# A hand-synchronised ring of two blocks, a looped TensorE program, and ScalarE sums in every block, for row skewness

## The chip, the cores and the metric

One core of a Trainium2 chip. The metric is the device time of one execution in microseconds (us); times quoted are medians of several executions, with their range. In the profile, PE is the matrix engine (TensorE), PEld its weight load, DVE is VectorE, ACT is ScalarE, POOL is GpSimd, SP the engine that issues the loads. All times inside an execution count from the start of the profile's span.

An execution more than 1.5% above the fastest of the same kernel is marked slow.

## The reference

```python
rows, cols = 1024, 8192                      # x, float32, normal
mean = np.mean(x, axis=-1, keepdims=True)
std = np.std(x, axis=-1, keepdims=True)
z = (x - mean) / (std + 1e-8)
return np.mean(z ** 3, axis=-1)              # 1024 numbers
```

The 33.5 MB of x are read once. From the three raw sums of a row (of x, x^2 and x^3) the result follows in a few small operations.

## The kernel before

Eight blocks of 128 rows by 8192 columns, each loaded in pieces. For every piece ACT squares (and sums the squares), DVE multiplies the square by x (and sums the cubes), and PE sums x: it transposes chunks of 128 columns, all added up in one PSUM tile `tp`; ACT copies that tile, and one more matmul with a column of 1/n gives the mean. A scheduler sets all waits and picks one of eight buffers for each piece.

```python
UNITS = [[4096, 4096], [4096, 4096], [4096, 4096], [4096, 4096],
         [3584, 2304, 2304], [2304, 2304, 2048, 1536],
         [1664, 1792, 1920, 1664, 1152],
         [1024, 1024, 1152, 1280, 1408, 1152, 1152]]
S1_ACT = {(0, 0): 1024, (1, 0): 1024, (2, 0): 1024}   # columns that ACT sums
X_BUFS = 8
# ...
for k, w in enumerate(widths):
    xt = xpool.tile([P, w], FP, tag="x", name=f"x_{b}_{k}")
    nc.sync.dma_start(out=xt, in_=xv[b, :, c0 : c0 + w])
    for s, e in _slices(w):                            # at most 2304 columns
        nc.scalar.activation(out=sq, in_=xt[:, s:e], func=AF.Square, scale=s_scale,
                             accum_out=s2u[:, j : j + 1])
        nc.vector.scalar_tensor_tensor(out=cube, in0=sq, scalar=1.0, in1=xt[:, s:e],
                             op0=ALU.mult, op1=ALU.mult, accum_out=s3u[:, j : j + 1])
    # ... ACT's sum, where S1_ACT has one
    for c in range(n):
        nc.tensor.matmul(out=tp, lhsT=xt[:, c * P : (c + 1) * P], rhs=ident,
                         start=..., stop=..., is_transpose=True)
nc.scalar.copy(out=tsb, in_=tp)                        # once a block
nc.tensor.matmul(out=s1ps[:, b : b + 1], lhsT=tsb, rhs=onesn, start=True, stop=True)
# ... the first six blocks are closed together, the last two on ACT, step by step
```

## Time and profile before

| | before |
|---|---|
| time, median (range) | 91.47 us (91.38 to 91.63), 4 runs |
| span of the profile | 89.7 us |
| 16 DMA engines busy with loads | 89.7% of the span |
| last piece landed | 83.56 us |
| last square on ACT ended | 84.72 us |
| last product on DVE ended | 87.20 us |
| ACT from its first to its last square | 69.0 us busy, 7.6 us idle |
| mean granted clock of PE | 0.978 |

The busy rows of the page cut the span into 40 slices, a digit for each (9 is 90% or more). A row of groups gives line, engine, operation, output<-inputs, count, then busy time and mean length in ns, then the idle time just before these instructions and what ended it. Landing times and the sizes of single packets come from the records in the trace; the row on ACT's busy and idle time was added up from its instruction records. The lines themselves stand in the prediction.

### The profile page before, as it was taken

The numbers are of one execution on the slowest core, as the hardware profiler recorded it, in microseconds if no ns is written. First come the engines' busy times: TensorE is split into PE (matmuls) and PEld (weight loads), VectorE is DVE, ScalarE is ACT, GpSimd is POOL, SyncE is SP. The second block draws the span as 40 slices with busy tenths as digits, with TensorE's granted clock in tenths as the row PEclk, the third lists the DMA queues.
The fourth block names the chain that finished last, engine by engine and source line by source line (L and its number), as shares of the span: only waits on it lengthen the run. The fifth ranks groups of instructions, "written<-read, shape, count | busy, mean of one in ns | idle before, by whom it ended". The sixth has DMA issues, their size and how long they took to land.

```text
span 89.7 us, 1368 instructions
## 1 busy us (share of the span) xinstructions
PE 64.9 (72%) x504; PEld 59.3 (66%) x504; DVE 72.7 (81%) x80; ACT 72.1 (80%) x106; POOL 11.3 (13%) x14
## 2 busy tenths in 40 slices
PE   0003999892882919989998988888987798969710
PEld 0003999791872909979897977877876787848500
DVE  1000498989999298995999999999999999999970
ACT  6003999699991999859898989978979898999950
POOL 3000000000000000000000000000005999900030
PEclk9999999999999997599999999999999999999998
DMA  3999999999999999999999999999999999994000
GB/s 117 351 424 438 424 431 431 431 431 424 446 416 431 424 438 424 424 438 427 415 409 418 419 427 419 421 415 419 409 414 417 404 413 411 421 412 161 0 0 2
DMA packets 4038, 33.64 MB, mean 375 GB/s; under 512 B 576, under 2 KB 576, under 8 KB 2240
## 3 DMA queue, kind: packets, MB, share of 16 engines
q1 hardware_dynamic: 4032, 33.56, 89.7%
q8 instruction: 4, 0.07, 0.3%
q14 instruction: 2, 0.02, 0.0%
HBM read 33.55 MB, written 0.00 MB: 374 GB/s over the span
## 4 chain that ended last, share of the span: by engine, by line
DMA 73%; ACT 13%; issue 5%; DVE 4%; SPq 1%; PE 1%; DVEq 0%; ACTq 0%
DMA x<-in_x_dram 73%; ACT sq L147 9%; DVE sq L152 3%; ACT sqps L147 1%; ACT same L159 1%; SPq L140 1%; PE s1ps L175 1%; ACT tsb L174 0%; ACT s3u L128 0%; ACT v L127 0%; ACT var L125 0%; DVE num L189 0%; ACT m1sq L124 0%; DVE skew L192 0%; ACT nm L126 0%
## 5 line engine op out<-in xcount | busy, mean ns | idle before, releaser
L152 DVE SCALAR_TENSOR_TENSOR sq<-sq,x 128x2048 f32<-128x2048 f32 (+9 forms) x35 | 70.7, 2071 | 13.4 <-ACT sq L147 13.3
L165 PE MATMUL tp<-ident,x 128*128 128x128 f32 x488 | 62.6, 288 | 17.3 <-DMA x<-in_x_dram 17.2
L165 PEld LDWEIGHTS tp<-ident,x 128*128 128x128 f32 x488 | 57.9, 150 | 20.9 <-DMA x<-in_x_dram 12.7
L147 ACT ACTIVATE sq<-x 128x2048 f32<-128x2048 f32 (+9 forms) x35 | 60.6, 1734 | 10.7 <-DMA x<-in_x_dram 9.9
L110 POOL TENSOR_TENSOR vara<-m2a,m1sqa 128x6 f32<-128x6 f32 x1 | 1.8, 1822 | 67.1 <-DVE m3a L99 67.1
L147 ACT ACTIVATION_READ_ACCUMULATOR sq<-x 128x1 f32 x35 | 6.5, 186 | 0.0
L175 PEld LDWEIGHTS s1ps<-onesn,tsb 128*128 128x128 f32 x16 | 2.4, 188 | 5.2 <-ACT tsb L174 5.2
L175 PE MATMUL s1ps<-onesn,tsb 128*128 128x1 f32 x16 | 3.1, 260 | 3.3 <-ACT tsb L174 3.3
L174 ACT COPY tsb<-tp 128x128 f32<-128x128 f32 x8 | 2.0, 256 | 2.0 <-PE tp L165 2.0
L114 POOL TENSOR_TENSOR rra<-vara,expo 128x6 f32<-128x6 f32 x1 | 3.3, 3267 | 0.0
L159 ACT ACTIVATE same<-x 128x1024 f32<-128x1024 f32 x3 | 3.1, 1041 | 0.0
L152 DVE DVE_READ_ACCUMULATOR sq<-sq,x 128x1 f32 x35 | 2.9, 83 | 0.0
L111 POOL TENSOR_TENSOR m1sq3a<-m1sq3a,vara 128x6 f32<-128x6 f32 x1 | 1.9, 1868 | 0.1
L77 ACT ACT_TABLE_LOAD x1 | 1.3, 1283 | 0.7 <-PEq L208 0.7
L187 POOL TENSOR_TENSOR rr<-var,expo 128x2 f32<-128x2 f32 x1 | 0.7, 702 | 7.7 <-ACT var L125 7.7
L152 DVE SCALAR_TENSOR_TENSOR cube<-sqps,x 128x1152 f32<-128x1152 f32 x1 | 1.4, 1350 | 0.0
L113 POOL TENSOR_TENSOR m3a<-m3a,m1sq3a 128x6 f32<-128x6 f32 x1 | 1.2, 1201 | 0.1
L147 ACT ACTIVATE sqps<-x 128x1152 f32<-128x1152 f32 x1 | 1.1, 1136 | 0.1
L115 POOL TENSOR_TENSOR skew<-m3a,rra 128x6 f32<-128x6 f32 x1 | 1.1, 1069 | 0.1
L124 ACT ACTIVATE m1sq<-s1ps 128x1 f32<-128x1 f32 x2 | 0.3, 171 | 0.5 <-PE s1ps L175 0.5
L75 DVE MEMSET onesn<- 128x1 f32 x1 | 0.1, 59 | 0.8 <-PEq L208 0.8
L112 POOL TENSOR_TENSOR m1sq3a<-m1sq3a,nm1a 128x6 f32<-128x6 f32 x1 | 0.7, 697 | 0.0
(28 smaller groups left out, 6.8 us busy)
## 6 DMA issues: line engine op xcount, KB each, us to landing
x<-in_x_dram SPq DMA_DIRECT2D x8, 2048.0 KB, 23.4
x<-in_x_dram SPq DMA_DIRECT2D x4, 1152.0 KB, 27.9
x<-in_x_dram SPq DMA_DIRECT2D x4, 576.0 KB, 8.6
x<-in_x_dram SPq DMA_DIRECT2D x1, 1792.0 KB, 33.0
x<-in_x_dram SPq DMA_DIRECT2D x2, 832.0 KB, 13.9
x<-in_x_dram SPq DMA_DIRECT2D x1, 1024.0 KB, 21.1
x<-in_x_dram SPq DMA_DIRECT2D x2, 512.0 KB, 10.0
x<-in_x_dram SPq DMA_DIRECT2D x1, 960.0 KB, 13.2
```

The source lines that it names most:

```text
L77: nc.scalar.activation(out=tiny, in_=onesn, func=AF.Square)
L110: g.tensor_tensor(out=var, in0=m2, in1=m1sq, op=ALU.subtract)
L111: g.tensor_tensor(out=m1sq3, in0=m1sq3, in1=var, op=ALU.add)
L113: g.tensor_tensor(out=m3, in0=m3, in1=m1sq3, op=ALU.add)
L114: g.tensor_tensor(out=rr, in0=var, in1=expo, op=ALU.pow)
L115: g.tensor_tensor(out=skew[:, 0:F], in0=m3, in1=rr, op=ALU.mult)
L147: nc.scalar.activation(out=sq, in_=xt[:, s:e], func=AF.Square, scale=s_scale, accum_out=s2u[:, j : j + 1],)
L152: nc.vector.scalar_tensor_tensor(out=cube, in0=sq, scalar=1.0, in1=xt[:, s:e], op0=ALU.mult, op1=ALU.mult, accum_out=s3u[:, j : j + 1],)
L159: nc.scalar.activation(out=same[:, 0:w_act], in_=xt[:, w - w_act : w], func=AF.Copy, scale=inv_n, accum_out=s1a[:, b : b + 1],)
L165: nc.tensor.matmul(out=tp, lhsT=xt[:, c * P : (c + 1) * P], rhs=ident, start=(k == 0 and c == 0), stop=(c0 == C and c == n - 1), is_transp ...
L174: nc.scalar.copy(out=tsb, in_=tp)
L175: nc.tensor.matmul(out=s1ps[:, b : b + 1], lhsT=tsb, rhs=onesn, start=True, stop=True)
```

## The change

Its intent: do away with the scheduler's waits and with most of PE's instruction stream. The whole of x passes through a ring of two blocks; every engine has one semaphore and a written order; PE runs a loop of four turns over two blocks (110 transposes, 55 a block) and gets "grants" from SP as pieces land. For the loop every block must look alike, so ACT sums the first 1152 columns of every block. Blocks 4 to 7 are cut into fewer pieces, and the closing of a block is rewritten.

```diff
-    [3584, 2304, 2304],
-    [2304, 2304, 2048, 1536],
-    [1664, 1792, 1920, 1664, 1152],
-    [1024, 1024, 1152, 1280, 1408, 1152, 1152],
+    [2304, 2944, 2944],
+    [2176, 1664, 2176, 2176],
+    [1920, 2304, 2304, 1664],
+    [1536, 1920, 1792, 1664, 1280],
 ]
-S1_ACT = {(0, 0): 1024, (1, 0): 1024, (2, 0): 1024}
-X_BUFS = 8
+S1_ACT = 1152
+RING = 2
+ISSUE_LAG = 6000
+PARTS = (
+    [4096, 6144, 7168, 8192],
+    [4096, 6144, 7168, 7680, 8192],
+)
... (a small class that records each engine's operations with the names they wait for)
+    for i, (b, u, s, e) in enumerate(slices):
+        k = units[u][1]
+        square(i)
+        cube(i)
+        pos = i - of_block[b][0]
+        if pos == (1 if b < 4 else 0):
+            first_sum(b)                      # ACT: 1152 columns
+        if b == F and pos == 1:
+            early_on_act()                    # ACT: needs m1a of blocks 4, 5
+        if b and b % RING == 0 and pos == 1 and b <= F:
+            means(b // RING - 1)              # DVE: makes m1a of two blocks
...
+        if i == of_block[b][-1]:
+            copy_sums(b)                      # ACT: needs PE's last part of b
...
+        with tensor.Fori(0, NB // RING):
+            for h in range(RING):
+                c0 = S1_ACT
+                for i, end in enumerate(PARTS[h]):
+                    tensor.sem_inc(more, -1)._wait_ge(more, 1)      # a grant
+                    for c in range(c0, end, P):
+                        t = nc.tensor.matmul(
+                            out=tp[h], lhsT=at(h, c, c + P), rhs=ident,
+                            start=c == S1_ACT, stop=c + P == C, is_transpose=True,
+                        )
+                    t.then_inc(pe, 1)
+                    c0 = end
+                    if h and i == 0:
+                        mean(0)
+            mean(1)
```

In the code F is 6, L is 7 and NB is 8; `m1a` holds the means of the first six blocks, and DVE fills it for two blocks at a time. A part of PARTS is granted when the piece that holds its last column has landed; a piece may be overwritten when its cubes, ACT's sum and PE's part are done.

## The prediction

An assumed time per grant is cut that went into the walk and so into its waits; an assumed stop of PE's loop is cut that stood with the third rival, whose 99 to 101 us now rest on PE's slow pace alone ("its clock" there is PE's).

> **What bounds the kernel now.** I read the page's busy tenths and chain first, then the groups, the waits, the DMA view, and the timeline of the first and last ten microseconds.
>
> ```profile
> DVE  1000498989999298995999999999999999999970
> ACT  6003999699991999859898989978979898999950
> PEclk9999999999999997599999999999999999999998
> DMA  3999999999999999999999999999999999994000
> ...
> DMA 73%; ACT 13%; issue 5%; DVE 4%; SPq 1%; PE 1%; DVEq 0%; ACTq 0%
> ```
>
> The DMA row is full from the second slice to the 36th, and the chain lies on loads for 73% of the span. The load stream is the bound: the last piece lands at 83.56 us (the trace's landing records). ACT and DVE are nearly as full, so the margin below the stream is small. PE's clock drops once, in the slices around 36 to 40 us.
>
> ```profile
> L152 DVE SCALAR_TENSOR_TENSOR sq<-sq,x 128x2048 f32<-128x2048 f32 (+9 forms) x35 | 70.7, 2071 | 13.4 <-ACT sq L147 13.3
> L165 PE MATMUL tp<-ident,x 128*128 128x128 f32 x488 | 62.6, 288 | 17.3 <-DMA x<-in_x_dram 17.2
> L147 ACT ACTIVATE sq<-x 128x2048 f32<-128x2048 f32 (+9 forms) x35 | 60.6, 1734 | 10.7 <-DMA x<-in_x_dram 9.9
> L174 ACT COPY tsb<-tp 128x128 f32<-128x128 f32 x8 | 2.0, 256 | 2.0 <-PE tp L165 2.0
> L159 ACT ACTIVATE same<-x 128x1024 f32<-128x1024 f32 x3 | 3.1, 1041 | 0.0
> ```
>
> What counts here is ACT's idle time. Of its 10.7 us before squares, 5.95 is the wait for the first piece (timeline), leaving 4.8; the copies add 2.0 and two small waits 0.8. Between 8.18 us and the end of the last square at 84.84, ACT therefore idles only some 7.5 us, nearly all of it waiting for data. This is the room that new ACT work can use.
>
> ```profile
> q1 hardware_dynamic: 4032, 33.56, 89.7%
> q8 instruction: 4, 0.07, 0.3%
> q14 instruction: 2, 0.02, 0.0%
> ```
>
> The four q8 packets have 16,384 bytes each and start at 26.3, 47.4, 65.2 and 80.9 us. They look negligible and are not. In the landing records of the piece before the first one, the median DMA engine lands at 22.33 and the last at 22.74; of the next piece, at 27.22 and 28.85. One engine lost 1.2 us to one packet and never won it back[...]. After 47.4 a second engine is 1.2 us late. At the end the median is 81.92 and the last 83.56.
>
> ```profile
> 83.58 1.14 ACT L147 ACTIVATE sqps<-x 128x1152 f32<-128x1152 f32 x1
> 84.84 0.27 ACT L174 COPY tsb<-tp 128x128 f32<-128x128 f32 x1
> 85.24 1.35 DVE L152 SCALAR_TENSOR_TENSOR cube<-sqps,x 128x1152 f32<-128x1152 f32 x1
> 86.44 0.29 ACT L128 ACTIVATE s3u<-v,nm 128x1 f32<-128x1 f32 x1
> 87.04 0.16 DVE L192 TENSOR_TENSOR skew<-num,rr 128x2 f32<-128x2 f32 x1
> 87.23 0.35 SPq L193 DMA_DIRECT2D out_dram<-skew  x1
> ```
>
> The last square starts 0.02 us after its data: ACT is just in time. The end costs 3.6 us after the last landing, up to the end of the last result at 87.20.
>
> [...] PE's 504 weight loads and 504 matmuls make about 1,010 instructions[...] and there are four packets. [...] here transposes are 117 ns apart when warm (32 in 3.71 us), but 214 at the start (28 in 5.99 us), and the drop near 36 us comes in a stretch where PE was 70% busy.
>
> **The change part by part.**
>
> *PE's loop.* One turn is 110 weight loads, 110 transposes, 9 grants and two means of 5 instructions: 239[...]. If it isn't fetched again the four packets go. That is worth 1.64 (81.92 to 83.56) less the 0.41 of natural spread: 1.2 us of landing time.
>
> *Loads.* Packets of 4,608 bytes take 181 ns and of 9,216 bytes 352, so 11 ns fixed and 0.0369 ns a byte; a piece costs an engine 8 x 11 + 9 = 97 ns beyond its bytes. 24 pieces for 27 save 0.3 us. The ring does hold fewer columns, but a place lies free about 6.6 us after its piece landed (two squares, two cubes)[...], and comes round only after 16,384 columns, 19.8 us. I find no starved queue. Estimated last landing: 83.56 - 1.2 - 0.3, about 82.1 to 83.0 (the walk below uses 83.0).
>
> *ACT's work.* From the rows by shape (2048: 1907 ns, 1152: 1155) a square costs 0.84 ns a column + 0.188 us, start to start. Between first landing and end of the last square, after:
> - 34 squares: 8 x 8192 x 0.84 ns + 34 x 0.188 = 61.4 us (36 before: 61.8)
> - 8 sums of 1152 columns at 1.155: 9.2 us (before 3 of 1024 at 1.048: 3.1)
> - 7 copies at 0.28: 2.0; first closing 0.45; six steps of block 6's closing 1.65
>
> The sum is 74.7 us against 69.0 before. Starting at 8.2, ACT can't finish its last square before 82.9 even if it never waits: it has become as long as the load stream.
>
> *ACT's waits.* I walked the four orders (ACT, DVE, PE, SP) of the changed program instruction by instruction, each starting when its engine is free and its waits are met, with the durations above, 1.041 ns a column + 0.10 us for a cube, 117 ns a transpose[...]. The same walk over the order of before, given its landings, ends at 87.36 where the trace has 87.20, so its sums hold to about 0.2 us. For after it gives:
> - Blocks 0 to 3: seven waits of 0.3 to 0.5 us, 2.9 in all. ACT now takes 9.1 us of the 9.9 us of a block.
> - End of block 4: 0.6 us at the copy, which waits for PE.
> - End of block 5: 1.8 us at the copy. The pieces end at 3840, 6016 and 8192, PE's parts at 4096, 6144, 7168, 7680, 8192, so the part to 6144 just misses the third piece, and 32 transposes (3.8 us and four grants) are left after the last one.
> - Block 6: 2.8 us. After the second square ACT needs `m1a` of blocks 4 and 5. On DVE it is queued behind the cube of that very square (2304 columns, 2.5 us). This follows from the order alone and can't be hidden.
>
> 8.2 + 74.7 + 2.9 + 0.6 + 1.8 + 2.8 = 91.0 for the end of the last square (84.84 before), although its data landed at 83.0.
>
> *The end.* Then 0.3 for the last step of block 6, 0.28 for the copy, 0.5 for the mean on PE, 0.6 to the variance, 0.75 for the power on GpSimd, 0.2 for the product: 93.6. DVE's last cube ends at 92.6 and isn't on the path. Before it was 87.2: 6.4 us more. The launch around it should stay as it was: 91.54 + 6.4 = 97.9. I add 0.3 because with 55 transposes a block everywhere PE is about 70% busy, as where its clock dropped, and a slow stretch delays a copy: 98.2.
>
> **The rivals.**
> - *The load stream stays the bound, and the change wins.* Landing 1.5 us earlier with an end of 3.6 to 4.5 us gives 90.0 to 91.0. For it speak the 73% of loads on the chain; against it ACT's sum of 74.7 us, which leaves no room for the end, and the waits above. It needs ACT never to wait.
> - *ACT is the bound but its waits are short* (PE and DVE come in time, 2.9 us of waits alone): 8.2 + 74.7 + 2.9 + 2.7 = 88.5, so 92.9. Against it: the order in block 6.
> - [...] its clock stays low. [...] 214 in place of 117 ns for one part of 23 transposes (2.2 us), reaches ACT through the copies: 99 to 101.
> - *The ring starves the loads.* Loads of block 7 wait for PE's parts and cubes of block 5; if ACT lags by 6 us they are late too. In the walk each is still issued about 11 us or more before it lands, so this costs nothing more.
>
> **Range and chances.** The largest uncertain terms are the three waits (5.2 us) and PE's clock (0 to 2.5 us). Half of the waits gone gives 95.6; a slow PE gives 100.5. The limit for "within 2%" is 93.4, which needs nearly all waits gone. Slower 0.89, same 0.06, faster 0.05.
>
> **What would show each step.** The q8 instruction packets are gone from the middle of the span, and the last landing comes at 82 to 83 us. ACT's sum group has 8 at 1.15 us. The waits show ACT's small square of `m1a` waiting 2.8 us for DVE, and the copies waiting for PE by 4 us or more in all. The last square starts 5 us or more after its data, and the chain shows ACT where it showed loads. It would be wrong if ACT's idle time within the stretch were under 4 us, if the loads landed after 85 us (then the ring is the cause), or if PE's loop stopped for its branch.

## The result

The changed kernel takes **99.63 us** (98.44 to 100.27, 4 runs) against 91.47 us. The ratio is 1.0847 (95% interval 1.0746 to 1.0947). A ratio here is the mean time of one kernel's fast runs over that of the other's of the same rounds, so it isn't quite the ratio of the quoted medians (1.0892). The result lies between the 95.6 and 100.5 that the prediction works out for its good and its bad case, 1.4 us above the predicted 98.2.

The page of the changed kernel, part 2 (busy tenths) and part 4 (the chain); a slow run, 100.27 us:

```profile
DVE  0000798989898949898999998899145909999960
...
ACT  6006999699969696999999979990398099999940
PEclk9999999999999999999999996559999975998555
DMA  4899999999999999999999999999999991000000
...
POOL 1%; ACT 1%; PE 1%; issue 0%; DVE 0%; DVEq 0%; POOLq 0%
```

The DMA row now ends in the 34th slice of a longer span, and behind it there are five slices of work without loads. The chain says little here: it breaks off at 93.38 us and so covers only the last 2.3 us (the shares add up to some 3%), so that it shows neither loads nor ACT as the bound, and the readings below rest on waits and timeline instead. ACT is busy from the fourth slice to the 38th but for shallow dips (the 6s in the row) and two holes, in slices 28 to 29 and 32. PE's clock drops in slices 25 to 27 and 33 to 34, and again at the end where PE has little to do; before it dropped once.

```profile
L343 PE MATMUL tp<-ident,ring 128*128 128x128 f32 x440 | 56.6, 292 | 28.6 <-PEq L341 28.4
L183 ACT ACTIVATE sq<-ring 128x2048 f32<-128x2048 f32 (+8 forms) x34 | 61.2, 1804 | 9.2 <-DMA ring<-in_x_dram 9.2
L200 ACT ACTIVATE same<-ring 128x1152 f32<-128x1152 f32 x8 | 9.2, 1152 | 0.0
L209 ACT COPY tsb<-tp 128x128 f32<-128x128 f32 x8 | 2.1, 260 | 4.8 <-PE tp L343 4.8
L228 ACT ACTIVATE m1sqa<-m1a 128x6 f32<-128x6 f32 x1 | 0.2, 208 | 2.7 <-DVE m1a L216 2.7
```

These are the groups that answer to those of before. The sums cost ACT 9.2 us where they cost 3.1. ACT's wait for data ahead of squares is 9.2 us, 5.96 of it for the first piece, so 3.3 us for all others. New are 4.8 us of waiting for PE at the copies and 2.7 us for DVE ahead of a small square that takes 0.2 us.

```profile
q1 hardware_dynamic: 3600, 33.56, 81.6%
q8 instruction: 1, 0.02, 0.1%
q14 instruction: 2, 0.02, 0.0%
```

In the queues (packets, MB, share of 16 engines) one of the four q8 packets is left; it has 16,384 bytes, starts at 31.3 us and takes 1.08 us. One is enough: in the landing records the last DMA engine comes 0.37 us after the median one for the piece before it (27.52 and 27.89) and 1.5 us after it for the next (32.44 and 33.92), and so to the end (81.98 and 83.45). The last landing is 83.45 us, against 83.56 before: the loads gained 0.1 us in all.

Lines picked from the timeline around blocks 5 and 6 (start, length, engine, line, operation, in brackets the idle time before and who ended it):

```profile
61.05 5.14 PE L343 MATMUL tp<-ident,ring 128*128 128x128 f32 x23 [3.60 <-PEq L341]
...
66.82 3.69 PE L343 MATMUL tp<-ident,ring 128*128 128x128 f32 x32 [0.41 <-PEq L341]
70.55 0.27 ACT L209 COPY tsb<-tp 128x128 f32<-128x128 f32 x1 [4.07 <-PE tp L343]
75.89 2.56 DVE L192 SCALAR_TENSOR_TENSOR sq<-sq,ring 128x2304 f32<-128x2304 f32 x1 [1.09 <-ACT sq L183]
78.37 0.15 DVE L216 TENSOR_TENSOR m1a<-s1ps,s1a 128x2 f32<-128x2 f32 x1
78.56 0.21 ACT L228 ACTIVATE m1sqa<-m1a 128x6 f32<-128x6 f32 x1 [2.71 <-DVE m1a L216]
```

PE stands idle for 3.6 us until the third piece of block 5 has landed (60.88 us), then takes 5.14 us for 23 transposes (the second block's 23 took 2.70), then 3.69 us for the other 32, and ACT, which had squared all of block 5 by 66.5, waits 4.07 us for it. Then the small square of `m1a` waits until the 2.56 us cube ahead of the sum is through.

And lines picked from the end:

```profile
91.59 1.25 ACT L183 ACTIVATE sq<-ring 128x1280 f32<-128x1280 f32 x1
93.03 0.24 ACT L209 COPY tsb<-tp 128x128 f32<-128x128 f32 x1
93.21 1.49 DVE L192 SCALAR_TENSOR_TENSOR sq<-sq,ring 128x1280 f32<-128x1280 f32 x1
94.74 0.70 POOL L292 TENSOR_TENSOR rr<-var,expo 128x2 f32<-128x2 f32 x1 [11.03 <-ACT var L252]
95.55 0.16 DVE L302 TENSOR_TENSOR skew<-num,rr 128x2 f32<-128x2 f32 x1 [0.28 <-POOL rr L292]
```

The last square starts 8.1 us after its data landed; before it was 0.02 us. From its end to the last product it takes 2.9 us (92.84 to 95.71), where the kernel before took 2.5.

### The profile page after: what moved, and what is told of

Same layout as the page of the kernel before. It is cut to its first block, busy times and chain, and to the rows that moved or that the text cites. A ratio compares the mean times of both kernels' runs of the same rounds, so it can differ in the third digit from the quotient of the medians.

```text
span 98.5 us, 1321 instructions
## 1 busy us (share of the span) xinstructions
PE 58.7 (60%) x456; PEld 56.0 (57%) x456; DVE 73.5 (75%) x79; ACT 76.9 (78%) x112; POOL 5.9 (6%) x14
## 5 line engine op out<-in xcount | busy, mean ns | idle before, releaser
L192 DVE SCALAR_TENSOR_TENSOR sq<-sq,ring 128x2048 f32<-128x2048 f32 (+8 forms) x34 | 72.3, 2164 | 20.7 <-ACT sq L183 20.5
L343 PE MATMUL tp<-ident,ring 128*128 128x128 f32 x440 | 56.6, 292 | 28.6 <-PEq L341 28.4
L343 PEld LDWEIGHTS tp<-ident,ring 128*128 128x128 f32 x440 | 53.5, 152 | 30.4 <-issue 30.4
L183 ACT ACTIVATE sq<-ring 128x2048 f32<-128x2048 f32 (+8 forms) x34 | 61.2, 1804 | 9.2 <-DMA ring<-in_x_dram 9.2
L200 ACT ACTIVATE same<-ring 128x1152 f32<-128x1152 f32 x8 | 9.2, 1152 | 0.0
L183 ACT ACTIVATION_READ_ACCUMULATOR sq<-ring 128x1 f32 x34 | 6.4, 188 | 0.0
L235 POOL TENSOR_TENSOR vara<-m2a,m1sqa 128x6 f32<-128x6 f32 x1 | 0.2, 197 | 77.2 <-ACT m1sq3a L229 77.2
L192 DVE DVE_READ_ACCUMULATOR sq<-sq,ring 128x1 f32 x34 | 2.8, 83 | 0.0
L200 ACT ACTIVATION_READ_ACCUMULATOR same<-ring 128x1 f32 x8 | 1.5, 189 | 0.0
L235 POOL TENSOR_TENSOR rra<-vara,expo 128x6 f32<-128x6 f32 x1 | 1.3, 1336 | 0.0
## 6 DMA issues: line engine op xcount, KB each, us to landing
ring<-in_x_dram SPq DMA_DIRECT2D x3, 1088.0 KB, 10.8
```

Source lines behind the costliest of these rows:

```text
L183: pr.op("act", ("sq", i), waits, lambda: act(out=sqs[i % SQ_BUFS][:, 0 : e - s], in_=at(b, s, e), func=AF.Square, scale=s_scale, accum_out ...
L192: pr.op("dve", ("cube", i), [("sq", i), "s3u"], lambda: dve.scalar_tensor_tensor(out=sq, in0=sq, scalar=1.0, in1=at(b, s, e), op0=ALU.mult ...
L200: pr.op("act", ("s1a", b), us + prev, lambda: act(out=same, in_=at(b, 0, S1_ACT), func=AF.Copy, scale=inv_n, accum_out=s1a[:, b : b + 1],))
L235: pr.op("pool", name, waits, lambda: g.tensor_tensor(out=out, in0=in0, in1=in1, op=op))
L343: t = nc.tensor.matmul(out=tp[h], lhsT=at(h, c, c + P), rhs=ident, start=c == S1_ACT, stop=c + P == C, is_transpose=True,)
```

## The experiments

Twelve kernels ran, each timed in three rounds beside the kernel before on the same chip. All give the right result but `no_sums`. The last column is the difference from the changed kernel's ratio, turned into us of 91.5. The change wasn't run again in these rounds, and the interval of its own ratio is 0.9 us either way, so a difference of less than about 1 us in that column can't be told from none.

| kernel | all runs, us (s: marked slow) | ratio to before | against the change |
|---|---|---|---|
| the change | 100.27s, 99.87, 99.39, 98.44 | 1.0847 | |
| means_first | 97.07, 96.93, 96.65, 97.49 | 1.0605 | -2.2 |
| piece_6144 | 99.17s, 97.52, 99.43s, 99.02s | none | unclear |
| piece_4096 | 99.19, 98.93, 98.86, 98.99 | 1.0813 | -0.3 |
| copy_late | 97.63s, 97.40, 97.86s, 96.07 | 1.0573 | -2.5 |
| sum_128 | 97.28, 97.63, 97.43, 97.52 | 1.0632 | -2.0 |
| no_sums | 98.18s, 98.16s, 96.52, 97.59 | 1.0593 | -2.3 |
| unrolled | 99.92s, 99.89s, 97.71, 100.10s | none | unclear |
| warm | 99.61, 99.58, 99.67, 99.84 | 1.0873 | +0.2 |
| before_sums | 93.42, 93.53, 93.38, 93.55 | 1.0195 | (on the kernel before) |
| means_copy | 95.47, 95.15, 94.84, 95.72 | 1.0397 | -4.1 |
| all_fixed | 94.24, 95.01, 94.24, 93.72 | 1.0297 | -5.0 |
| all_fixed_512 | 93.18, 93.92, 94.28, 94.43 | 1.0285 | -5.1 |

### means_first: the wait for DVE

```diff
         square(i)
-        cube(i)
         pos = i - of_block[b][0]
+        if b and b % RING == 0 and pos == 1 and b <= F:
+            means(b // RING - 1)
+        cube(i)
...
-        if b and b % RING == 0 and pos == 1 and b <= F:
-            means(b // RING - 1)
```

> The sum of the means of blocks 4 and 5 on DVE (m1a) is put before the second cube of block 6 instead of behind it; nothing else. Theory (ACT is the bound, its waits add to the end): the 2.7 us wait of ACT's small square for DVE goes and the whole of it comes off the end: 99.6 - 2.7 = about 96.9 us (95.5 to 98.0 with the spread of PE's clock). Rival (the ring or the load stream sets the end): nothing over 0.5 us.

Measured: 97.0 us, 2.6 us less by the medians and 2.2 by the ratios. The group of the small square, in the profile:

```profile
L228 ACT ACTIVATE m1sqa<-m1a 128x6 f32<-128x6 f32 x1 | 0.2, 199 | 0.0
```

Its 2.7 us of idle time are gone, and most of them came off the end. What ACT waits for here sets the end, and an order of two instructions on DVE was worth over 2% of the time.

### piece_6144 and piece_4096: why PE is late in block 5

```diff
-    [2176, 1664, 2176, 2176],
+    [2176, 1664, 2304, 2048],      # piece_6144
+    [2176, 1920, 1920, 2176],      # piece_4096
```

> Block 5 is cut at 2176, 3840, 6144, 8192, so that PE's part to 6144 no longer misses the third piece: the reason that the prediction gave for the 1.8 us wait at the end of block 5. If that reason holds: about 1.5 us faster, 98.1. Rival: PE is late because its first part ends at 4096 and so starts only with the third piece, after which 55 transposes stand without a gap; then the cut changes nothing: 99.6 within 0.7.

> Block 5 is cut at 2176, 4096, 6016, 8192, so that PE's first part starts with the second piece. By the rival reason of the run before, PE is 0.7 us or more nearer to its data, and it idles 2.4 us less ahead of that part, so that its clock need not drop (it took 5.1 us for 23 transposes where 2.7 is usual): the wait of 4.1 us at the copy falls to 1 to 2 us, and the time to 96.7 to 97.5 us. If PE's clock drops all the same: 98.9.

Of piece_6144 only one run counts as fast, so its time settles nothing. Its profile (99.17 us, slow) does: PE's 23 transposes start at 61.61, end at 65.98, and the 32 others follow without a gap. The earlier grant found PE still at work, so a cut at 6144 couldn't bring it forward. The prediction's reason for the wait is wrong.

With the cut at 4096 PE's work is in another order; its timeline:

```profile
55.38 6.20 PE L343 MATMUL tp<-ident,ring 128*128 128x128 f32 x55 [0.68 <-PEq L341]
...
64.40 5.06 PE L343 MATMUL tp<-ident,ring 128*128 128x128 f32 x32 [2.71 <-PEq L341]
```

The 23 transposes of block 5 now run on behind block 4's, as the rival said, and the wait at the copy falls to 1.40 us. But PE then waits for the last piece, and it is the 32 transposes that run slowly (5.06 us for 3.69). Another copy, in block 2, waited 2.8 us in this run. So the time of 98.96 us is what was expected for the case that the clock drops all the same (98.9; 0.88 was granted on average); the gain of 0.3 us is within the noise.

### copy_late: the waits at the copies

```diff
-        if i == of_block[b][-1]:
+        if b and pos == 0:              # behind the first square of block b
+            copy_sums(b - 1)
+            if b - 1 >= F:
+                pending = close_on_act(b - 1)
+        if i == of_block[L][-1]:
             copy_sums(b)
-            if b >= F:
-                pending = close_on_act(b)
+            pending = close_on_act(b)
```

> ACT copies the sums of a block behind the first square of the next block instead of ahead of it, so that ACT doesn't stand still while PE finishes. Theory: the waits at the copies (0.7 and 4.1 us in the profiled run) are hidden by the square: 99.6 - 3.5 = about 96.1 us (95.5 to 97), with less spread from run to run, since PE's clock then hardly reaches ACT. Rival (PE's lag counts anyway, through the places that it frees and the loads that follow): less than 1 us.

Measured: 97.5 us by the median, 2.5 us less by the ratio (96.7 us as mean of its two fast runs). The wait view of its profile (engine, line <- who: us in total, times, longest; a slow run):

```profile
ACT tsb L209 <- PE tp L346: 1.9, 1, 1.9
```

One wait of 1.9 us is left, for block 5, where PE is over 3 us late, more than a square can hide. So the gain is about two thirds of what was expected; the expectation that the scatter would shrink was wrong (96.07 to 97.86).

### sum_128 and no_sums: ACT's own sums

```diff
-S1_ACT = 1152
+S1_ACT = 128                       # sum_128
```
```diff
-        pr.op("act", ("s1a", b), ...)        # no_sums: the sums away,
+        pr.marks["s1a", b] = pr.marks["s1a0"]
+    pr.op("dve", "s1a0", [], lambda: dve.memset(s1a, 0.0))
```

> ACT sums 128 columns of each block instead of 1152, PE's loop has 126 transposes instead of 110. It takes 6.9 us of work from ACT and gives 8 transposes more a block to PE. Theory A (ACT's own sums are the whole of the loss): 99.6 - 5.8 = about 94 us. Theory B (ACT mostly waits for others by now, and PE takes longer with each block, so that the room is turned into longer waits at the copies: 2.1 and 2.9 us by the walk with warm PE, and 0.8 us a block for data): only 0.8 to 2 us, 97.5 to 98.8.

> The changed kernel without ACT's sums (s1a is set to zero on DVE; the result is wrong on purpose, as 1152 columns are missing from each mean). PE's work and all waits stay. This takes 9.2 us of work from ACT, and, unlike sum_128, gives PE nothing more. Theory (by now ACT stands behind PE and DVE in blocks 4 to 6, so what it saves ahead of them it waits there): 99.6 - 2.1 = about 97.5 us (96.5 to 98.5), with the waits at the copies 1.5 to 2 us longer than the 4.8 us of the changed kernel. Rival (the sums are the loss): 93 or less.

Both times land where the second theory put them: 97.48 us (-2.0, at the edge of the range) and, with PE's work unchanged, 97.88 us (-2.3 by the ratio). 9.2 us of work less on ACT bring 2.3 us. Where the rest went stands in the waits of no_sums (a slow run, as the profiled one of the change):

```profile
ACT sq L184 <- DMA ring<-in_x_dram: 11.5, 7, 5.9
ACT tsb L206 <- PE tp L340: 8.4, 5, 3.7
ACT m1sqa L225 <- DVE m1a L213: 2.7, 1, 2.7
```

The copies wait 8.4 us instead of 4.8 (3.6 more, where 1.5 to 2 were expected), the squares 11.5 instead of 9.2, the small square 2.7 as ever. Added up from the records between first and last square, ACT is busy 65.0 us and idle 16.7, where the changed kernel has 73.7 and 10.8: two thirds of the saved work has become waiting. ACT was no longer the engine that everything waits for; it took turns with PE and DVE.

### before_sums: the same kind of sum in the kernel before

```diff
+            if b >= nw and k == 0:          # blocks 3 to 7; the result is not used
+                nc.scalar.activation(
+                    out=same, in_=xt[:, 0:1024], func=AF.Copy, scale=inv_n, accum_out=spare,
+                )
```

> The kernel before with one sum more on ACT in each of blocks 3 to 7 (1024 columns, the result not used), PE's work as it was: 5.2 us of ACT work alone. Theory (ACT is full at the end, so the sums of the last blocks count): 91.46 + 1.9 = 93.3 us (92.8 to 93.8) by the same walk. Rival (ACT waits for data 7.5 us, the sums fit in there): under 0.5 us.

Measured: 93.47 us, ratio 1.0195 (1.0171 to 1.022), so 1.8 us, by the walk 1.9. In a kernel where ACT idles 7.6 us, 5.2 us of work on it still cost a third of themselves. (Not all of this idle time is waiting for data, as the expectation has it: 4.8 us are, 2.0 are waits of the copies for PE.) The chain of this run fits with that:

```profile
ACT 37%; DMA 33%; issue 12%; PE 7%; DVE 5%; SPq 3%; DVEq 0%; ACTq 0%
```

The chain was on loads for 73% before; with the sums it is on loads for a third and on ACT for more.

### unrolled and warm: PE's loop and PE's clock

```diff
-        with tensor.Fori(0, NB // RING):
+        for _ in range(NB // RING):                # unrolled
```
```diff
+                    if i < 2:                      # warm, ahead of a grant
+                        for _ in range(8):
+                            nc.tensor.matmul(out=idle, lhsT=ident, rhs=ident,
+                                             start=True, stop=True, is_transpose=True)
                     tensor.sem_inc(more, -1)._wait_ge(more, 1)
```

> PE's loop is written out, all else the same. One instruction packet of 16 KB is left with the loop and has made one DMA engine 1.1 us late; written out there should be four. As one packet already costs what four cost (each meets another engine), the last landing stays at 83.4 us within 0.3 and the time at 99.6 within 0.8. Rival (the loop's branch or a refetch stops PE): 1 us or more faster. Rival (the packets matter): landing 1 us later.

> In each block PE does eight transposes of the identity into a place that nobody reads ahead of its first and of its second grant, where it would stand idle: 3.7 us more work a turn. Theory (PE's clock drops because PE is 60% busy): the granted clock rises from 0.90 to 0.95 or more, the waits at the copies fall by 2 us or more, the time to 97.0 to 98.0. Rival (the clock has another cause, or the extra work delays PE as much): 99.6 or slower.

Written out, three runs took 99.9 to 100.1 us and one 97.71, so the time can't be told from the loop's (only one run counts as fast). The queue:

```profile
q8 instruction: 3, 0.05, 0.2%
```

Three packets (I had expected four), a last landing of 83.82 us against 83.45 with one packet and 83.56 with the four of the kernel before. So each packet beyond the first cost 0.4 us or nothing. In the landing records of the kernel before, the packet at 47.4 us made a second engine late rather than the late one later: of the 16 engines the last three bring the next piece at 49.39, 50.60 and 50.75 us, and brought the one before it at 46.45, 46.62 and 47.83. The loop neither wins nor loses anything that can be seen.

Warm did what it was meant to do to the clock, 0.95 for 0.90, and nothing to the time, 99.64 us. Its clock row and the line of block 5:

```profile
PEclk9999999999999999999999999589999999999755
...
61.09 4.22 PE L351 MATMUL tp<-ident,ring 128*128 128x128 f32 x23 [2.74 <-PEq L349]
```

The drop that the changed kernel has in slices 33 to 34 is gone, the one at 61 us (slices 26 to 27 here) is not: PE still had to wait 2.74 us for the third piece there, and 23 transposes took 4.22 us. The copy of block 5 waited 3.4 us. So the mean clock is a poor measure here; what costs is one drop in the one place where ACT waits for PE, and filling other gaps didn't help it.

The clock records of the traces of the kernel before and of the changed one show where the drops come, which the mean hides. Before, the clock was half from 34.62 to 38.03 us (and from 89.23, after PE's last work); in the changed kernel from 59.70 to 66.53, from 80.18 to 83.60 and from 90.42 on. In the 3.41 us (the length of the shortest of these) ahead of the drops at 34.62, 59.70, 80.18 and 90.42 PE was busy 40%, 34%, 30% and 32% of the time; in warm it worked 1.04 of the 3.77 us ahead of 61.09 us, 28%. Yet as idle a stretch elsewhere brought none: from 31.20 to 34.60 us in the changed kernel, with most of the 3.32 us of idle time before 34.09 us in it, PE worked 0.51 us, 15%, and the clock stayed full to 59.70. So a gap alone doesn't settle it; what does was not shown.

### means_copy, all_fixed and all_fixed_512: the repairs together

all_fixed is means_copy (both orders above) with two blocks cut so that PE's first part starts with the second piece:

```diff
-    [2176, 1664, 2176, 2176],
+    [2176, 1920, 1920, 2176],
...
-    [1536, 1920, 1792, 1664, 1280],
+    [1792, 2304, 1536, 1408, 1152],
```

all_fixed_512 sets `S1_ACT = 512` on top, 120 transposes a turn.

> The means of blocks 4 and 5 ahead of the second cube of block 6, and the copies behind the next block's first square: the two waits that cost most, both away. If they are separate costs on ACT's way, their gains add up: 99.6 - 2.6 - 2.1 = about 94.9 us (94 to 96). If the one was hidden behind the other, about 97.

> As means_copy, with blocks 5 and 7 cut so that a piece ends at 4096 (2176, 1920, 1920, 2176 and 1792, 2304, 1536, 1408, 1152): PE's first part starts with the second piece. ACT still sums 1152 columns a block. The walk gives 0.8 us less than means_copy: 93.0 to 94.5 us. Theory: ACT's own work (74.7 us from 8.2 us on, and 2.7 us of waits for data) now sets the end, so it stays over the kernel before by 1.5 us or more. Rival (only the waits made it slower): 91.5 or less.

> As all_fixed, with ACT summing 512 columns and PE's loop at 120 transposes. The walk gives the same time as all_fixed within 0.3 us (PE's end takes the place of ACT's): 92.5 to 93.8. If ACT's sums alone were left as a cost: 4.3 us of work less, 91 or less, which would beat both kernels.

The gains of the two orders nearly add up: 2.2 and 2.5 alone, 4.1 together. The cuts bring another 0.9, which is within the scatter (95% intervals of the ratios 1.0349 to 1.0446 and 1.0231 to 1.0364). With 512 columns on ACT the time stays where it was (1.0285 for 1.0297); its median of 94.1 us is above the 92.5 to 93.8 that I had expected. No version beats the kernel before. In all_fixed ACT idles only 5.2 us between first and last square, but is busy 73.2 us (69.0 before), and its last square ends at 86.83 us instead of 84.72. In all_fixed_512 it is busy 70.0 us and the last square ends at 85.77; in both, the last landing is as before (83.61 and 83.40 us). What a version without any late landing engine would do was not tried.

## Why the prediction was right

**ACT becomes the bound.** Right as an account of when ACT's last square ends, though ACT alone is not the bound (see the sums below). The prediction had that end at 91.0. Measured in the profiled run: start 8.36, 73.7 of work, 10.8 of waits, end 92.85. Term by term:

| term | predicted | measured |
|---|---|---|
| ACT's work from first to last square | 74.7 | 73.7 |
| waits in blocks 0 to 3 | 2.9 | 3.3 |
| copy of block 4 | 0.6 | 0.7 |
| copy of block 5 | 1.8 | 4.1 |
| small square behind DVE in block 6 | 2.8 | 2.7 |
| end of last square to last product | 2.6 | 2.9 |

The sum of the four separate waits (4.1 + 0.7 + 2.7 + 3.3 = 10.8) is the whole of ACT's idle time. In blocks 0 to 3 there were four waits of 0.8 to 1.0 us rather than seven of 0.3 to 0.5. The size that was off is the copy of block 5, by 2.3 us, more than the 1.4 us between the predicted time and the median: PE ran at half pace at that very place (5.14 us for 23 transposes, 2.70 for those at 50.22 us), in this profile of a slow run. The work, put 1.0 us too high, hid a part of it, which is luck. The prediction had put 0.3 us in the sum for it and a slow part of 23 transposes (2.2 us) among the rivals, up to 99 to 101 us. That rival came true beside the main story, by PE's clock (0.50 from 59.70 to 66.53 us). Its ground for the 0.3 us, that PE is about 70% busy as where its clock dropped, was too coarse: in the kernel before, PE was busy 40% in the 3.41 us just ahead of that drop (31.21 to 34.62 us).

One reading of the kernel before was wrong without harm: of ACT's 7.5 us of idle time not "nearly all" but 4.8 us were waiting for data. And one announced sign did not come: the chain doesn't show ACT where it showed loads, as it breaks off at 93.38 us.

**The reason given for the wait of block 5** was wrong: "the part to 6144 just misses the third piece". PE's first part ends at 4096 and the second piece at 3840, so PE starts block 5 only with the third piece, and then has 55 transposes ahead of it without a gap. piece_6144 and piece_4096 show it in PE's timeline. With the cut at 4096 the time moved by 0.3 us, within the noise; with that at 6144 it can't be told.

**"The four packets go"** and with them 1.2 us of landing: wrong. One stayed, and with one the last engine is 1.5 us behind the median at the end (81.98 and 83.45), with four 1.6 (81.92 and 83.56). The last landing came at 83.45 us, past the range of 82 to 83. This step failed without any effect on the time, as the loads no longer set it; had the rival of the load stream been true, it would have failed by this term.

**The sums as a cost** were right in sign and wrong as an account. The prediction put their 6.1 extra us into ACT's work as if all of it came off the end again when taken away. no_sums and sum_128 show 2.3 and 2.0 us, for 9.2 and 6.9 us of work taken away. On the kernel before 5.2 us of sums cost 1.8. When several engines are nearly full, a term of a sum is what stands in the way at that place, not what its removal brings.

**The ring starves nothing**: right as far as the trace shows. The DMA row is full from the third slice to the 33rd, the last landing is no later than before.

**The branch of PE's loop**: no stop shows. The third turn starts at 50.22, as soon as its piece has landed (50.05), and the fourth 0.16 us after the second mean. The loops of the runs differ in length, 241 instructions here (counted from the code), 273 in sum_128 and 305 in warm; each of the three profiles has one q8 packet of 0.02 MB in the whole run.

What stays open: why the time differs from run to run of one kernel (96.07 to 97.86 us for copy_late, at mean clocks of 0.891 to 0.908); no reason is shown, as only one run of each kernel was traced. And what causes the last 2.7 us between all_fixed and the kernel before: its last square ends 2.1 us later, and from there to the last product it takes 2.8 us for 2.5, but all_fixed_512, with 3.2 us less of ACT's work, is no faster by its ratio. The ring in place of eight buffers, the fewer pieces and the rewritten closing were never tried alone.

## What to carry to other kernels

When one resource sets the time and two engines stand a few per cent below it, count the work of those engines from their first to their last instruction, not as a share of the span; a change that fills their gaps makes each of their waits count, and then the order of two small instructions (4.1 us in means_copy) can cost more than a whole class of work (2.3 us in no_sums). Walk the written order of each engine with traced durations before building: a small instruction that waits for one queued behind a long instruction, which itself waits for the first engine, shows on paper. To learn what a part costs, take it away: here 9.2 us of work were worth 2.3 us.
